# A decoder layer whose first product runs on x before its norm's root is known

## The chip, the cores and the metric

The kernel runs on one core of one Trainium2 chip. A core has TensorE (PE, matrix products and transposes, results in PSUM banks), VectorE (DVE), ScalarE (ACT) and GpSimd (POOL), which run side by side, each through its own instructions in order, and wait for one another by semaphores. SyncE (SP) issues most transfers between the chip's memory and the on-chip memory; ACT and POOL issue some. The metric is the device time of one execution in microseconds (us), the median of several.

## The reference, cut to what matters

One layer of a hybrid decoder: 256 prompt rows and 8 rows of new tokens, 2048 wide. Both start with a root-mean-square norm, and the normed rows go through one wide product, whose columns are split among attention, the gates and a state-space (SSM) branch:

```python
def rms_norm(x, w):
    y = x * lax.rsqrt(jnp.mean(x * x, axis=-1, keepdims=True) + EPS)
    return y * w

def token_mixers(hn, ...):            # hn = rms_norm(x, norm_mix_pre)
    proj = jnp.einsum('bld,de->ble', hn, lw['w_in'])
    q, k, v, z, xbc, dt_raw, gates = jnp.split(proj, SPLITS, axis=-1)
    xbc_act, new_conv = causal_conv(xbc, conv_in, conv_w, conv_b)    # columns X, B and C
    dt = softplus(dt_raw + dt_bias); a = -exp(a_log)                 # decays
    ...
```

The root of a row is one number for that row. So (x w r) W = r ((x w) W): it can be put on the product's result. The columns called B (1024 of them, for 8 groups) are the first that the kernel computes, 512 at a time, then C, then the 64 columns of dt (in 128), then X.

## The kernel before, in words

**Layout.** Activations stand transposed: a chunk is 128 of the 2048 channels on the partitions by 264 columns (256 prompt rows and 8 sample rows). There are 16 chunks. Products are of fp32 accuracy from parts: an operand is split into a high part, rounded to fp32r (a cast on ACT), and a low part, the difference (a subtraction on DVE). Each 128 x 128 block of weights then takes three matmuls: high by high (L192), high by the low part of x (L195), low by high (L196).

**The helper `gemm` (L147 to L198)** computes 512 columns: for each four chunks it loads 1 MB of raw weights (tile `raw`, 3 buffers, SP's queue, L163), casts `hi` and `lo` in halves of 1024 elements (L178 and L180 when they are tied behind given instructions, else L182 and L183; 4 buffers each), and runs 24 matmuls for each half, into four PSUM banks of tag `g` (5 banks; small transposes use 3 banks of tag `s`). One product of 512 columns is 192 matmuls.

**The start.** x comes in rows, in halves of 1024 columns (L230); sample rows, identity and norm vector go by ACT's queue (L231 to L233), small vectors by POOL's. In a block whose order is kept as written for PE, ACT and DVE (L265 to L304): idle matmuls on zeros (`busy`), transposes of x by fours (`turn`, L275), of the norm vector (L285) and the sample rows (L287), copies of the results into `XR` (L283, L290, L292, L297), sums of squares (L279, L281, L288, L293), the root by Newton steps on DVE (helper `rsqrt`, L98 to L116), and its broadcast over partitions by transposes (L302). Then each chunk is normalised: `xf = XR * w_pre * root` on DVE (L310), `XH` a cast on ACT (L92), `XL` on DVE (L93). The first product (columns B) runs on them, its weight casts tied behind the chunks' (L312, L313).

**What sets the order.** Outside the kept block a scheduler orders each engine's instructions by priorities and buffers; weight loads and casts get a higher priority, so they run ahead as far as buffers come free. `tc.issue_after` ties an instruction behind another. `mm0` holds the first product's matmuls; small vectors are transposed behind mm0[16] (L319 to L329).

**After the first product**, `conv` (L339 to L351) takes each result by ACT and DVE, `decays` (L353) computes a product of 128 columns and a long chain on its 64 rows, with a result that goes out to memory and comes back broadcast (tile `bc`, L482 to L488). It is called after the first product of B. The SSM branch (L499 and on) uses it after the products of C and X.

Of the kernel before, what the change touches and what calls it, by code (L numbers as in the profile page):

```python
# [32 lines left out]
def build(tc, I, O, wbufs=(3, 4, 4), gbufs=5, sbufs=((3,), (1,), (3,)), woff=0, aux="gpsimd", rr=1.4, pr=1.2, su=2, sr=1.0, hb=5, xbb=2, x0g=(0, 1, 2, 3), x0st="sync"):  # L33
    nc = tc.nc
    V, S, G, PE = nc.vector, nc.scalar, nc.gpsimd, nc.tensor
    dma, st = nc.sync.dma_start, nc.gpsimd.dma_start
# [226 lines left out]
    V.memset(ss, 1.0)
    ET = mybir.EngineType
    with tc.manual_schedule(engines={ET.PE, ET.Activation, ET.DVE}):  # L265
        pw = sps()
# [5 lines left out]
        def turn(t, k):
            ps = gps()
            for c in range(4 * k, 4 * k + 4):
                PE.transpose(ps[:, (c % 4) * P:(c % 4 + 1) * P], xts[t][:, c * P:(c + 1) * P], ident)  # L275
            return XR[:, 4 * k:4 * k + 4, t * P:(t + 1) * P], ps[:, :].rearrange("p (c n) -> p c n", c=4)

        busy(7)
        S.activation(sq[:NS], xts[2][:NS], AF.Square, accum_out=ss[:NS, 2:3])  # L279
        for h in range(2):  # L280
            S.activation(sq[:, h * XC:h * XC + XC], xts[0][:, h * XC:h * XC + XC], AF.Square, accum_out=s4[:, h:h + 1])  # L281
            for k in (2 * h, 2 * h + 1):
                V.tensor_copy(*turn(0, k))  # L283
# [6 lines left out]
        S.copy(XR[:, :, NP:T], pn[:, 128:256].rearrange("p (c n) -> p c n", c=16))  # L290
        for k in range(2):
            S.copy(*turn(1, k))  # L292
        V.tensor_tensor_reduce(sv2, xts[1][:, XC:], xts[1][:, XC:], 1.0, 0.0, ALU.mult, ALU.add, s4[:, 3:4])  # L293
        s2 = s4.rearrange("p (t h) -> p t h", t=2)
        V.tensor_tensor(ss[:, 0:2], s2[:, :, 0], s2[:, :, 1], ALU.add)
        for k in range(2, 4):
            xr_end = S.copy(*turn(1, k))  # L297
# [1 line left out]
        rs = rsqrt(cp, [(lambda a: a, ss)], P, 3, 1.0 / D, EPS, "rx")
        rbx = gps()  # L300
        for t, n in enumerate((P, P, NS)):
            PE.transpose(rbx[:, t * P:t * P + n], rs[:n, t:t + 1].broadcast_to([n, P]), ident[:n, :n])  # L302
        busy(2)
        rbx = rbx[:, :T]  # L304
# [2 lines left out]
    first = {0: xr_end.ins}, {}
    for c in range(16):
        xf = til(A0, [P, T], "xf", 3)
        V.scalar_tensor_tensor(xf, xrs[c], w_pre[:, c:c + 1], rbx, ALU.mult, ALU.mult)  # L310
        a, b = split(xf, XH[c], XL[c])
        first[0][c + 1] = a.ins  # L312
        first[1][c - 1] = b.ins  # L313
# [39 lines left out]
    def decays():  # L353
# [72 lines left out]
    for g in range(8):  # L426
        if g % 4 == 0:
            for nm, c0 in (("B", C_B), ("C", C_C)):
                pss = pss0 if g == 0 and nm == "B" else gemm(win, [(c0 + g * P, 512)], 16, X)
                for i in range(4):  # L430
                    cid = (c0 - C_X) // P + g + i
                    t = til(A2, [P, NP], "bc" + nm, 5)
                    conv(pss[i], cid, t)
# [730 lines left out]
```

## Time and profile before

| | before |
|---|---|
| median of 3 runs | 2142.59 us (2141.12 to 2143.07) |
| the profiled execution | 2147.37 us, of it the span 2145.6 us |
| mean granted clock of TensorE | 0.995 |
| PE, DVE, ACT busy | 99%, 64%, 52% |

Line numbers such as L192 are those of the kernel before. A tile's name stands without its buffer number. In the timeline a row is start, busy time, engine, line, operation, output and inputs, shape, count, and in brackets how long the engine stood idle before it and what ended that; rows of the same kind that follow one another are joined, with their count. "128*128 128x264" on a matmul is the weight block and the moving operand. The span's start is 0.

### The profile page before, as it was taken

To read this page: it belongs to the slowest core of one execution; us is meant where nothing else is said; L and a number is where in the kernel's file an instruction comes from. 1 tells how busy PE (TensorE), PEld (TensorE's weight loads), DVE (VectorE), ACT (ScalarE), POOL (GpSimd) and SP (SyncE) were. 2 spreads that over 40 slices of the span, in tenths; PEclk is the share of its full clock that TensorE was granted. 3 is DMA by queue.
4 is the path that set the end of the run, shared out by engine and by line. 5 is a ranking of instruction groups with operands and counts; after the bars stand their busy time and mean duration, and the time that the engine had idled before them with its cause. 6 is when DMAs were issued, how large, how long until landed. Compare 5 with 4: busy or idle time off the path is not lost.

```text
span 2145.6 us, 43115 instructions
## 1 busy us (share of the span) xinstructions
PE 2116.6 (99%) x17512; PEld 2083.6 (97%) x17512; DVE 1369.1 (64%) x2748; ACT 1105.0 (52%) x1969; POOL 234.2 (11%) x462
## 2 busy tenths in 40 slices
PE   8999999999999999999999999999999999999997
PEld 8999999999999999989999999999999999999997
DVE  7877777777689988867544554755455455544444
ACT  6555555555579877755533444554444444434442
POOL 1111011110123321233001100000000000000000
PEclk9999999999999999999999999999999999999998
DMA  7665655565577787787568975556555555565553
GB/s 254 208 195 191 192 192 177 192 192 192 190 259 251 254 287 252 266 280 260 179 208 183 219 256 184 167 186 206 193 188 188 190 195 195 185 212 177 177 177 100
DMA packets 214999, 442.50 MB, mean 206 GB/s; under 512 B 12000, under 2 KB 25840, under 8 KB 214280
## 3 DMA queue, kind: packets, MB, share of 16 engines
q1 hardware_dynamic: 192800, 370.91, 53.5%
q0 software_dynamic: 21664, 68.64, 9.7%
q8 instruction: 137, 2.24, 0.4%
q14 instruction: 62, 0.51, 0.1%
q10 hardware_dynamic: 336, 0.21, 0.0%
HBM read 402.81 MB, written 41.45 MB: 207 GB/s over the span
## 4 chain that ended last, share of the span: by engine, by line
PE 91%; DMA 5%; DVE 2%; issue 1%; ACT 1%; SPq 0%; POOL 0%; DVEq 0%; ACTq 0%; POOLq 0%
PE g L192 28%; PE g L196 28%; PE g L195 28%; DMA raw<-in_w_attn_branch 1%; DMA out_ssm_sample<-h 1%; DMA h<-in_state_ssm 1%; DMA ta_d<-tg 0%; PE w L735 0%; ACT hi L182 0%; PE w L728 0%; DMA xt<-in_x_prompt 0%; PE w L696 0%; PE s L499 0%; DMA raw<-in_w_in 0%; DVE lo L183 0%
## 5 line engine op out<-in xcount | busy, mean ns | idle before, releaser
L183 DVE TENSOR_TENSOR lo<-raw,hi 128x1024 fp32r<-128x1024 f32 (+1 forms) x632 | 765.4, 1214 | 595.5 <-ACT hi L182 594.2
L182 ACT CAST hi<-raw 128x1024 fp32r<-128x1024 f32 (+1 forms) x632 | 657.5, 1043 | 867.5 <-PE g L195 788.2
L192 PE MATMUL g<-XH,hi 128*128 128x264 f32 x2192 | 624.4, 288 | 2.3 <-ACT hi L182 1.1
L195 PE MATMUL g<-XL,hi 128*128 128x264 f32 x2192 | 622.0, 286 | 0.0
L196 PE MATMUL g<-XH,lo 128*128 128x264 f32 x2192 | 619.7, 287 | 1.7 <-DVE lo L183 1.0
L192 PEld LDWEIGHTS g<-XH,hi 128*128 128x128 f32 x2192 | 410.7, 188 | 6.9 <-issue 2.4
L195 PEld LDWEIGHTS g<-XL,hi 128*128 128x128 f32 x2192 | 411.4, 188 | 4.2 <-issue 3.5
L196 PEld LDWEIGHTS g<-XH,lo 128*128 128x128 f32 x2192 | 408.9, 188 | 5.3 <-issue 1.9
L195 PE MATMUL g<-HL,hi 128*128 128x264 f32 x1408 | 397.6, 284 | 0.0
L196 PE MATMUL g<-HH,lo 128*128 128x264 f32 x1408 | 397.0, 284 | 0.0
L192 PE MATMUL g<-HH,hi 128*128 128x264 f32 x1408 | 393.7, 285 | 0.0
L195 PEld LDWEIGHTS g<-HL,hi 128*128 128x128 f32 x1408 | 266.0, 189 | 0.9 <-DVE HL L956 0.8
L196 PEld LDWEIGHTS g<-HH,lo 128*128 128x128 f32 x1408 | 263.9, 188 | 0.0
L192 PEld LDWEIGHTS g<-HH,hi 128*128 128x128 f32 x1408 | 261.1, 188 | 0.0
L192 PE MATMUL g<-FH,hi 128*128 128x264 f32 x704 | 200.9, 286 | 0.0
L196 PE MATMUL g<-FH,lo 128*128 128x264 f32 x704 | 200.4, 285 | 0.0
L195 PE MATMUL g<-FL,hi 128*128 128x264 f32 x704 | 199.2, 283 | 0.0
L195 PE MATMUL g<-YL,hi 128*128 128x264 f32 x512 | 145.9, 286 | 0.8 <-DVE YL L93 0.8
L196 PE MATMUL g<-YH,lo 128*128 128x264 f32 x512 | 146.3, 287 | 0.0
L192 PE MATMUL g<-YH,hi 128*128 128x264 f32 x512 | 145.2, 288 | 0.9 <-ACT YH L92 0.9
L195 PEld LDWEIGHTS g<-FL,hi 128*128 128x128 f32 x704 | 132.8, 189 | 0.0
L192 PEld LDWEIGHTS g<-FH,hi 128*128 128x128 f32 x704 | 132.5, 188 | 0.0
(438 smaller groups left out, 2966.1 us busy)
## 6 DMA issues: line engine op xcount, KB each, us to landing
raw<-in_w_in SPq DMA_DIRECT2D x136, 1024.0 KB, 5.3
raw<-in_w_gate_up SPq DMA_DIRECT2D x88, 1024.0 KB, 5.1
raw<-in_w_down SPq DMA_DIRECT2D x44, 1024.0 KB, 5.1
raw<-in_w_ssm_branch SPq DMA_DIRECT2D x32, 1024.0 KB, 5.5
h<-in_state_ssm POOLq DMA_DIRECT2D x64, 256.0 KB, 5.7
out_ssm_sample<-h POOLq DMA_DIRECT2D x64, 256.0 KB, 5.2
raw<-in_w_attn_branch SPq DMA_DIRECT2D x32, 512.0 KB, 10.6
raw<-in_w_out SPq DMA_DIRECT2D x16, 1024.0 KB, 5.3
```

What stands on the lines that cost most here:

```text
L182: S.copy(hi[:, :, :w], r)
L183: V.tensor_tensor(lo[:, :, :w], r, fr(hi[:, :, :w]), ALU.subtract)
L192: ins = PE.matmul(ps[m][:, :T], wh, XH[kc], start=f, stop=False)
L195: PE.matmul(ps[m][:, :T], wh, XL[kc], start=False, stop=False)
L196: PE.matmul(ps[m][:, :T], wl, XH[kc], start=False, stop=l)
```

## The change

x is loaded by column pieces of 512 (both 128-row blocks in one transfer), laid between the first product's weight pieces. The block of kept order now holds the whole first product. After the idle matmuls, two chunks are transposed, and then a loop over eight passes b takes two chunks each: 16 matmuls with the high weights (4 result banks, 2 chunks, high and low part of x times w_pre, not normed), and after the first and the second bank's four a `turn` of a chunk of the next pass; then 8 matmuls with the low weights. `put` makes the two parts straight from the transposes' bank (ACT, then DVE), `keep_x` copies the raw chunk to `XR` (DVE for the odd chunks below 10, else ACT). Squares are summed for each piece behind passes 0 to 3 (ACT and DVE). Behind pass 4 the root is made: sums on DVE, a square root on ACT, a reciprocal and one Newton step on DVE, broadcast by transposes on PE and a copy on ACT (`rbs`). Behind passes 5 to 7 the chunks are normalised, two a pass, for the products that follow; behind the last one more, then the four results are scaled by the root (`BU`), then the rest. `decays` is called after the first product of C instead of B. The table that ACT loads at the start is the one of Sqrt, not Exp.

```diff
-    S.activation(warm, warm, AF.Exp)
+    S.activation(warm, warm, AF.Sqrt)
...
-    XC = 1024
-    for t in range(2):
-        for c0 in range(0, D, XC):
-            dma(xts[t][:, c0:c0 + XC], I["x_prompt"][t * P:t * P + P, c0:c0 + XC])
-    S.dma_start(xts[2][:NS], I["x_sample"])
...
+    load_x(0)
+    S.dma_start(xs8[:NS], I["x_sample"])
     S.dma_start(ident, I["consts"][:, 0:P])
     S.dma_start(N1[0:16], I["norm_mix_pre"].rearrange("(c p) -> c p", p=P))
+    load_raw(0, 2)
+    load_x(1)
+    load_x(2)
+    load_raw(1, 1)
+    load_x(3)
+    load_raw(2, 1)
...
+        def turn(c):
+            ps = sps()
+            for t in range(2):
+                PE.transpose(ps[:, t * P:t * P + P], xp[:, t, c * P:(c + 1) * P], ident)
+            PE.transpose(ps[:, NP:T], xs8[:NS, c * P:(c + 1) * P], ident[:NS, :NS])
+            return ps
+
+        def put(c, ps):
+            H, L = XU[c]
+            S.mul(H, ps[:, :T], w_pre[:, c:c + 1])
+            V.scalar_tensor_tensor(L, ps[:, :T], w_pre[:, c:c + 1], fr(H), ALU.mult, ALU.subtract)
+            return c, ps
+
+        def keep_x(c, ps):
+            (V.tensor_copy if c % 2 and c < 10 else S.copy)(XR[:, c, :], ps[:, :T])
...
+        def norm(c):
+            xf = til(A0, [P, T], "xf", 2)
+            V.scalar_tensor_tensor(xf, XR[:, c, :], w_pre[:, c:c + 1], rbs, ALU.mult, ALU.mult)
+            split(xf, XH[c], XL[c])
...
+        for b in range(8):
+            lo = low(b, hi)
+            for m in range(4):
+                for k in range(2):
+                    for x in range(2):
+                        mm = PE.matmul(pss0[m][:, :T], hi[:, k, m * P:(m + 1) * P], XU[2 * b + k][x], start=b + k + x == 0, stop=False)
...
+                if m < 2 and b < 7:
+                    a = put(2 * b + 2 + m, turn(2 * b + 2 + m))
+                    if m == 0:
+                        hi2 = high(b + 1)
+                    keep_x(*a)
+            for m in range(4):
+                for k in range(2):
+                    PE.matmul(pss0[m][:, :T], lo[:, k, m * P:(m + 1) * P], XU[2 * b + k][0], start=False, stop=b + k == 8)
+            hi = hi2
+            if b < 4:
...
+                S.activation(sq[:, 0:512], xb[:, 0], AF.Square, accum_out=s4[:, 0, b:b + 1])
+                V.tensor_tensor_reduce(sq[:, 1024:1536], xb[:, 1], xb[:, 1], 1.0, 0.0, ALU.mult, ALU.add, s4[:, 1, b:b + 1])
+            if b == 0:
+                load_raw(3, 1)
+            if b == 4:
+                V.tensor_reduce(ss[:, 0:2], s4, mybir.AxisListType.X, ALU.add)
...
+                S.activation(rs, rx, AF.Sqrt)
+                V.tensor_scalar(rh, rx, -0.5, None, ALU.mult)
+                V.reciprocal(rs, rs)
+                V.tensor_tensor(rt, rs, rs, ALU.mult)
+                V.tensor_tensor(rt, rt, rh, ALU.mult)
+                V.scalar_tensor_tensor(rs, rt, 1.5, rs, ALU.add, ALU.mult)
+                rbx = sps()
+                for t, n in enumerate((P, P, NS)):
+                    PE.transpose(rbx[:, t * P:t * P + n], rs[:n, t:t + 1].broadcast_to([n, P]), ident[:n, :n])
+                S.copy(rbs, rbx[:, :T])
+            if b > 4:
+                for _ in range(2):
+                    norm(todo.pop(0))
+        norm(todo.pop(0))
+        for i in range(4):
+            V.tensor_tensor(BU[:, i, :], pss0[i][:, :T], rbs, ALU.mult)
+        pss0 = [BU[:, i, :] for i in range(4)]
+        for c in todo:
+            norm(c)
...
-    pss0 = gemm(win, [(C_B, 512)], 16, (XH, XL), behind=first)
...
-                if g == 0 and nm == "B":
+                if g == 0 and nm == "C":
                     dtT, tokm, ac, DF, dcol, dc1 = decays()
```

PE in the middle of the first product, before (XH and XL are the two parts of a normed chunk, hi and lo those of weights, g the result banks):

```order
L195 MATMUL g_350<-XL_9_91,hi_357 128x264
L196 MATMUL g_347<-XH_8_90,lo_358 128x264
L192 MATMUL g_347<-XH_10_92,hi_357 128x264
L195 MATMUL g_347<-XL_11_93,hi_357 128x264
L196 MATMUL g_347<-XH_10_92,lo_358 128x264
L196 MATMUL g_348<-XH_8_90,lo_358 128x264
L192 MATMUL g_348<-XH_10_92,hi_357 128x264
L195 MATMUL g_348<-XL_11_93,hi_357 128x264
L196 MATMUL g_348<-XH_10_92,lo_358 128x264
L196 MATMUL g_349<-XH_8_90,lo_358 128x264
```

Matmuls of the three kinds follow one another with nothing between them.

The same place after the change (xu2H and xu2L are the parts of the raw chunk 2 times w_pre, s a bank for transposes, xp and xs the rows of x):

```order
L338 MATMUL g_223<-xu2H_178,hi_258 128x264
L338 MATMUL g_223<-xu2L_179,hi_258 128x264
L338 MATMUL g_223<-xu3H_180,hi_258 128x264
L338 MATMUL g_223<-xu3L_181,hi_258 128x264
L293 MATMUL s_298<-ident_67,xp_134 128x128 x2
L294 MATMUL s_298<-ident_67,xs_43_135 128x8
L338 MATMUL g_224<-xu2H_178,hi_258 128x264
L338 MATMUL g_224<-xu2L_179,hi_258 128x264
L338 MATMUL g_224<-xu3H_180,hi_258 128x264
L338 MATMUL g_224<-xu3L_181,hi_258 128x264
```

The matmuls are the same in number; the order goes bank by bank with high weights, and the turns of the next pass's chunks now stand between them.

PE at the end of pass 4 after the change (rxy is the root; before, these transposes stood ahead of the product):

```order
L348 MATMUL g_225<-xu9H_192,lo_424 128x264
L348 MATMUL g_226<-xu8H_190,lo_424 128x264
L348 MATMUL g_226<-xu9H_192,lo_424 128x264
L368 MATMUL s_478<-ident_67,rxy_470 128x128 x2
L368 MATMUL s_478<-ident_67,rxy_470 128x8
L338 MATMUL g_223<-xu10H_194,hi_436 128x264
L338 MATMUL g_223<-xu10L_195,hi_436 128x264
```

The root's transposes stand behind the pass's low matmuls and ahead of the whole of pass 5.

ACT at the end of the first product, before:

```order
L92 CAST XH_22_104<-xf_319 128x264
L178 CAST hi_473<-raw_467 128x1024
L92 CAST XH_24_106<-xf_323 128x264
L92 CAST XH_26_108<-xf_327 128x264
L178 CAST hi_527<-raw_525 128x1024
L92 CAST XH_28_110<-xf_331 128x264
L92 CAST XH_30_112<-xf_335 128x264
L178 CAST hi_531<-raw_525 128x1024
L182 CAST hi_669<-raw_667 128x2x128
```

Each weight cast stands behind the two chunks before it, and the next product's casts (hi_669 on) come last.

The same after the change (hi_749, hi_753 and hi_807 are weights of the next product, s_539 and s_552 the banks of the turned chunks 14 and 15):

```order
L299 ACTIVATE xu14H_202<-s_539,w_pre_165 128x264
L308 CAST hi_545<-raw_290 128x1024
L182 CAST hi_749<-raw_747 128x1024
L182 CAST hi_753<-raw_747 128x1024
L182 CAST hi_807<-raw_805 128x1024
L304 COPY XR_172<-s_539 128x264
L299 ACTIVATE xu15H_204<-s_552,w_pre_165 128x264
L304 COPY XR_172<-s_552 128x264
```

Three casts of the next product's weights moved in ahead of the copy of chunk 14 and the high part of chunk 15.

DVE at the same place after the change (lo_750 to lo_812 belong to the next product; BU are the scaled results):

```order
L313 TENSOR_TENSOR lo_583<-raw_290,hi_545 128x1024
L318 SCALAR_TENSOR_TENSOR xf_609<-XR_172,w_pre_165,s6t_123 128x264
L183 TENSOR_TENSOR lo_750<-raw_747,hi_749 128x1024
L183 TENSOR_TENSOR lo_754<-raw_747,hi_753 128x1024
L183 TENSOR_TENSOR lo_808<-raw_805,hi_807 128x1024
L93 TENSOR_TENSOR XL_13_95<-xf_609,XH_12_94 128x264
L318 SCALAR_TENSOR_TENSOR xf_613<-XR_172,w_pre_165,s6t_123 128x264
L183 TENSOR_TENSOR lo_812<-raw_805,hi_811 128x1024
L93 TENSOR_TENSOR XL_15_97<-xf_613,XH_14_96 128x264
L318 SCALAR_TENSOR_TENSOR xf_617<-XR_172,w_pre_165,s6t_123 128x264
L93 TENSOR_TENSOR XL_17_99<-xf_617,XH_16_98 128x264
L375 TENSOR_TENSOR BU_128<-g_223,s6t_123 128x264
```

Each xf is now followed by its own XL, with only low casts between, where before two chunks' steps stood between the two.

## Rows read from the trace of the kernel before

**Rows 1.** The page's busy shares, and its chain of waits by engine

```profile
PE 2116.6 (99%) x17512; PEld 2083.6 (97%) x17512; DVE 1369.1 (64%) x2748; ACT 1105.0 (52%) x1969; POOL 234.2 (11%) x462
...
PE 91%; DMA 5%; DVE 2%; issue 1%; ACT 1%; SPq 0%; POOL 0%; DVEq 0%; ACTq 0%; POOLq 0%
```

**Rows 2.** Stretch, length, busy PE, PEld, DVE, ACT, POOL, granted clock, DMA share, GB/s

```profile
16.40:41.00 24.60, 23.87 (x190) 23.11 (x191) 22.33 (x47) 13.21 (x26) 0.00 (x0) 1.00 0.59 214
```

**Rows 3.** Waits of 0 to 120 us: total, times, longest

```profile
PE g L302 <- DVE rxy L115: 1.2, 1, 1.2
PE g L192 <- ACT hi L182: 1.1, 1, 1.1
...
PE g L196 <- DVE lo L180: 0.7, 1, 0.7
```

**Rows 4.** Timeline of the start, 0 to 18 us

```profile
1.40 1.28 ACT L79 ACT_TABLE_LOAD   x1 [1.40 <-PEq L1156]
...
1.88 0.44 ACTq L233 DMA_DIRECT2D N<-in_norm_mix_pre  x1
...
9.20 1.15 PE L287 MATMUL s<-ident,xt 8*128 8x8 f32 x16
...
10.58 1.23 DVE L293 CUSTOM_DVE_ANT_0 sv<-xt 128x1024 f32<-128x1024 f32 x1 [0.19 <-DMA xt<-in_x_prompt]
...
13.23 0.16 DVE L115 SCALAR_TENSOR_TENSOR rxy<-rxt,rxy 128x3 f32<-128x3 f32 x1
...
16.38 0.75 PE L192 MATMUL g<-XH,hi 128*128 128x264 f32 x4
```

**Rows 5.** Tiles N and xt, from issue to landing

```profile
DMA to landing us min/median/max: 5.8/5.8/5.8
...
DMA to landing us min/median/max: 4.3/6.3/8.4
```

**Rows 6.** Timeline of PE in the first product

```profile
33.43 0.65 PE L192 MATMUL g<-XH,hi 128*128 128x264 f32 x4
33.92 0.65 PE L195 MATMUL g<-XL,hi 128*128 128x264 f32 x4
```

**Rows 7.** Timeline of PE around transposes between matmuls

```profile
74.07 0.28 PE L196 MATMUL g<-XH,lo 128*128 128x264 f32 x1
74.28 0.27 PE L386 MATMUL s<-ident,dtT 64*128 64x64 f32 x1
...
74.71 0.28 PE L195 MATMUL g<-XL,hi 128*128 128x264 f32 x1
...
110.52 0.29 PE L195 MATMUL g<-XL,hi 128*128 128x264 f32 x1
110.64 0.38 PE L457 MATMUL s<-ident,xs 128*128 128x128 f32 x2
...
110.98 0.28 PE L192 MATMUL g<-XH,hi 128*128 128x264 f32 x1
```

**Rows 8.** Timeline of ACT in the first product

```profile
33.38 0.41 ACT L92 CAST XH<-xf 128x264 fp32r<-128x264 f32 x1 [0.94 <-DVE xf L310]
33.70 1.05 ACT L178 CAST hi<-raw 128x1024 fp32r<-128x1024 f32 x1
```

**Rows 9.** Timeline of DVE in the first product

```profile
32.85 0.89 DVE L310 SCALAR_TENSOR_TENSOR xf<-XR,w_pre,g 128x264 f32<-128x264 f32 x2
33.65 0.78 DVE L93 TENSOR_TENSOR XL<-xf,XH 128x264 fp32r<-128x264 f32 x2
34.34 1.23 DVE L180 TENSOR_TENSOR lo<-raw,hi 128x1024 fp32r<-128x1024 f32 x1
```

**Rows 10.** Timeline of DVE and PE where the decays are used

```profile
83.19 0.41 DVE L401 COPY y<-s 64x256 f32<-64x256 f32 x1
...
92.07 1.66 DVE L488 TENSOR_SCALAR bc<-bc,ac 128x128 f32<-128x128 f32 x8 [0.79 <-DMA bc<-acT_d]
...
130.58 0.44 PE L499 MATMUL s<-bc,X 128*64 128x128 f32 x4
```

More of the change, by code (lines that the diff above doesn't have):

```diff
@@ L220, in build @@
     RS = til(RSp, [P, 4, NS, 48], "RS")
+    BU = til(RSp, [P, 4, T], "BU")
     A0 = pool("a0")
@@ L224, in build, with load_x, load_raw @@
     G.memset(wz, 0.0)
-    xts = [til(A0, [P, D], f"xt{t}") for t in range(3)]
+    xp = til(A0, [P, 2, D], "xp")
+    xs8 = til(A0, [P, D], "xs8")
     N1 = til(A0, [P, P], "N1")
-    XC = 1024
-    for t in range(2):
-        for c0 in range(0, D, XC):
-            dma(xts[t][:, c0:c0 + XC], I["x_prompt"][t * P:t * P + P, c0:c0 + XC])
-    S.dma_start(xts[2][:NS], I["x_sample"])
+    xv = I["x_prompt"].rearrange("(t p) d -> p t d", t=2)
+    raws = []
+    def load_x(k):
+        dma(xp[:, :, 512 * k:512 * k + 512], xv[:, :, 512 * k:512 * k + 512])
+    def load_raw(g, parts):
+        raws.append(til(wp, [P, 4, 512], "raw", wbufs[0]))
+        n = 4 // parts
+        for h in range(parts):
+            k0 = 4 * g + n * h
+            dma(raws[g][:, n * h:n * h + n, :], win[k0 * P:(k0 + n) * P, C_B:C_B + 512].rearrange("(k p) n -> p k n", p=P))
+    load_x(0)
+    S.dma_start(xs8[:NS], I["x_sample"])
     S.dma_start(ident, I["consts"][:, 0:P])
     S.dma_start(N1[0:16], I["norm_mix_pre"].rearrange("(c p) -> c p", p=P))
+    load_raw(0, 2)
[4 more added lines that the diff above has]
+    load_raw(2, 1)
     VR = til(A0, [P, P], "VR")
@@ L257, in build @@
     ss = til(cp, [P, 3], "ss")
-    s4 = til(cp, [P, 4], "s4")
+    s4 = til(cp, [P, 2, 4], "s4")
     XR = til(A0, [P, 16, T], "XR")
-    xrs = [XR[:, c, :] for c in range(16)]
     sq = til(A0, [P, D], "sq")
-    sv2 = til(A0, [P, XC], "sv2")
+    XU = [[til(A0, [P, T], f"xu{c}{x}", 1, F32R) for x in "HL"] for c in range(16)]
+    rbs = s6t.rearrange("p b c -> p (b c)")[:, 0:T]
     V.memset(ss, 1.0)
@@ L270, in busy @@
                 PE.matmul(pw[:, 0:NP], wz[:, 0:P], wz, start=True, stop=True)
[L272 to L283, printed above, removed]
@@ L284, in build @@
-        pn = sps()
+        def turn(c):
[9 more added lines that the diff above has]
+            return c, ps
@@ new lines, in keep_x, with high, low @@
+        def keep_x(c, ps):
+            (V.tensor_copy if c % 2 and c < 10 else S.copy)(XR[:, c, :], ps[:, :T])
+        def high(b):
+            hi = til(wp, [P, 2, 512], "hi", wbufs[1], F32R)
+            S.copy(hi, raws[b // 2][:, 2 * (b % 2):2 * (b % 2) + 2, :])
+            return hi
+        def low(b, hi):
+            lo = til(wp, [P, 2, 512], "lo", wbufs[2], F32R)
+            V.tensor_tensor(lo, raws[b // 2][:, 2 * (b % 2):2 * (b % 2) + 2, :], fr(hi), ALU.subtract)
+            return lo
@@ L285, in build @@
+        def norm(c):
+            xf = til(A0, [P, T], "xf", 2)
+            V.scalar_tensor_tensor(xf, XR[:, c, :], w_pre[:, c:c + 1], rbs, ALU.mult, ALU.mult)
+            split(xf, XH[c], XL[c])
+        S.activation(sq[:NS], xs8[:NS], AF.Square, accum_out=ss[:NS, 2:3])
+        busy(9)
+        pn = gps()
         PE.transpose(pn[:, 0:16], N1[:16], ident[:16, :16])
-        for c in range(16):
-            PE.transpose(pn[:, 128 + 8 * c:136 + 8 * c], xts[2][:NS, c * P:(c + 1) * P], ident[:NS, :NS])
@@ L288, in build @@
-        S.activation(sq[:, :XC], xts[1][:, :XC], AF.Square, accum_out=s4[:, 2:3])
         S.copy(w_pre, pn[:, 0:16])
[L290 to L297, printed above, removed]
@@ L298, in build @@
-        busy(3)
[L299 to L304, printed above, removed]
+        pss0 = [gps() for _ in range(4)]
+        xs = [put(c, turn(c)) for c in range(2)]
+        busy(3)
+        hi = high(0)
+        for a in xs:
+            keep_x(*a)
+        todo = list(range(16))
@@ new lines, in build @@
+        for b in range(8):
[4 more added lines that the diff above has]
+                        mm = PE.matmul(pss0[m][:, :T], hi[:, k, m * P:(m + 1) * P], XU[2 * b + k][x], start=b + k + x == 0, stop=False)
+                        if b == 1:
+                            mm0.append(mm.ins)
+                if m < 2 and b < 7:
+                    a = put(2 * b + 2 + m, turn(2 * b + 2 + m))
+                    if m == 0:
+                        hi2 = high(b + 1)
+                    keep_x(*a)
+            for m in range(4):
[3 more added lines that the diff above has]
+            if b < 4:
+                xb = xp[:, :, 512 * b:512 * b + 512]
+                S.activation(sq[:, 0:512], xb[:, 0], AF.Square, accum_out=s4[:, 0, b:b + 1])
[4 more added lines that the diff above has]
+                V.tensor_reduce(ss[:, 0:2], s4, mybir.AxisListType.X, ALU.add)
+                rx, rh, rt, rs = (til(cp, [P, 3], "rx" + k) for k in "xhty")
+                V.tensor_scalar(rx, ss, 1.0 / D, EPS, ALU.mult, ALU.add)
+                S.activation(rs, rx, AF.Sqrt)
[11 more added lines that the diff above has]
+                    norm(todo.pop(0))
@@ L305, in build @@
+        norm(todo.pop(0))
[4 more added lines that the diff above has]
+            norm(c)
     for c in range(0, 16, 4):
         st(xT_d[c:c + 4].rearrange("c p t -> p c t"), XR[:, c:c + 4, :])
[L307 to L313, printed above, removed]
@@ L318, in build @@
     ps = sps()
-    with tc.issue_after(mm0[16]):
+    with tc.issue_after(mm0[8]):
         for k in range(5):
@@ L326, in build @@
     ps = sps()
-    with tc.issue_after(mm0[16]):
+    with tc.issue_after(mm0[8]):
         PE.transpose(ps[:, 0:48], VR[:48], ident[:48, :48])
@@ L366, in decays @@
         V.scalar_tensor_tensor(e, u, -1.0, u, ALU.mult, ALU.max)
-        S.activation(e, e, AF.Exp, scale=-1.0)
+        e_act = S.activation(e, e, AF.Exp, scale=-1.0)
         V.tensor_scalar(s, e, 2.0, None, ALU.add)
@@ L378, in decays @@
         na = til(cp, [P, 1], "na")
-        S.activation(na[h_], hv[h_, 1:2], AF.Exp)
+        with tc.issue_after(e_act.ins):
+            S.activation(na[h_], hv[h_, 1:2], AF.Exp)
         V.tensor_scalar(na[h_], na[h_], -1.0, None, ALU.mult)
```

## The prediction

> **What bounds the kernel now.** I read the busy shares and the chain of waits first. TensorE is busy 99% of the span and makes up 91% of the chain that ended last [rows 1], so only three things can move the time: work added to or taken from PE's queue, a wait of PE, or the time at which PE starts real work. Next I read the table by stretches. From 16.4 to 41 us, the first product (192 matmuls), PE is busy 23.87 of 24.60 us, DVE 22.33 and ACT 13.21 at a granted clock of 1.00 [rows 2]: DVE is nearly as full as PE, so vector work added in this stretch soon stops PE. PE's waits of the first 120 us are short: 1.2 for the root, 1.1 and 0.7 for weights [rows 3]. The timeline of the start shows what stands ahead of the product: transposes and the root on DVE, and the first product matmul at 16.38 [rows 4].
>
> The sum is made against the profiled run, 2147.37 us (span 2145.6 and 1.8 around it). That is 4.8 above the median 2142.59 of the runs; at the end I take 4.8 off.
>
> **A: the start, -5.5.** The first transpose of the change needs the norm vector, the identity and the first column piece of x. The vector is issued at 1.88 [rows 4] and lands 5.8 later [rows 5]: 7.7. The x landings are 4.3 to 8.4 from issue [rows 5]; the first piece is issued first, so it is there at about the same time. Then 0.3 for the vector's transpose, two turns of 0.62 each (worked out in B): 9.25. On ACT, H of the second chunk, 0.41, and the high cast of the weights, 1.05, one behind the other [rows 8]: about 10.9 for the first product matmul, where 16.38 stood. Ends: -5.0 (first piece late by the median landing) and -5.8.
>
> **B: turns inside the product, +8.7, and root transposes, +0.6.** Matmuls of the product start 0.49/4 = 0.122 us apart [rows 6]. Fourteen turns now stand between them, each two transposes of 128 rows and one of the 8 sample rows. Two 128-row transposes put between matmuls stretch 110.52 to 110.98, which is 0.46 where two intervals would be 0.24: 0.22 extra [rows 7]. A lone transpose from 64 rows stretches 74.07 to 74.71, which is 0.64 against 0.24: 0.40 extra [rows 7]. The 8-row transposes among themselves took 1.15/16 = 0.07 each [rows 4]. So a turn costs between 0.22 + 0.07 = 0.29 and 0.22 + 0.40 = 0.62; times 14, 4.1 to 8.7. I take the upper end, because the 64-row row is the only one in which a short transpose stands between full matmuls, as here. The three root transposes were ahead of the product and are now in it: 0.3 to 0.9, I take 0.6.
>
> The row with 64 rows shows 0.40 us lost around one short transpose. The Trainium skill, TensorEngine Tiling (Array Packing), Key Properties, says that a change of tiling mode (other than a change of tile within it) drains TensorE. By it each 8-row transpose would cost like that row, and the sum would be as here; without it the turns cost 4.1 and the sum is 4.6 less. The trace agrees so far, with 0.40 against 0.11 for each of the 128-row ones.
>
> **C: the root after the fifth pass, +0.9.** Root transposes stand in PE's order behind the low matmuls of pass 4 and wait for DVE's last root instruction. Ahead of it on DVE, once the low cast of pass 4 is done: two L of 0.45 with a copy 0.35 and an H 0.41 on ACT between them, a reduction and a scaling (0.4), the Sqrt on ACT (0.25), then four small ones of 0.16 [rows 4] with their handing over, 0.8 (all estimates from that row's size): 3.1 in all. PE covers 8 x 0.122 = 0.98 of it, so 2.1 at most. At least 0, if DVE is far ahead. Per pass DVE's path is 0.45 + 0.40 + 0.41 + 0.45 + 0.36 + 0.69 (half of the 1.23 square plus its read [rows 4]) + 1.22 (low cast [rows 9]) = 4.0, PE's is 24 x 0.122 + 2 x 0.62 = 4.17; DVE starts about 2 us ahead, gains 0.2 a pass, and so covers about half: 0.9.
>
> In that path ACT's H, DVE's L and the copy of the same transposed chunk stand one behind another; no row of before shows three readers of one bank. The Trainium skill, PSUM — Partial Sum Buffer, section "PSUM bank collisions raise a hardware error", says that two engines, readers too, must not be at one bank and the same partitions at once, so a program has to order them. By it the path is the 4.0 above; without that order DVE would need its own 3.2 only and term C would be nothing, 0.9 off the sum.
>
> **D: DVE behind the root, +7.0.** This is the large term. From the root to the first of the four scalings BU, DVE has 7 low casts of 1.23, some 0.1 of it under the next one [rows 9], = 7.9 (four of them already of the next product), four L at 0.40 = 1.6, four small vectors 1.0 (estimate: under the 0.40 of a chunk each), seven chunks of norm at 0.40 + 0.35 = 0.75 (0.80 and 0.69 for two [rows 9]) = 5.2, one BU 0.4: 16.1. To it come waits in the order shown in the last order piece: each norm's own low part waits for ACT's cast of the same chunk (0.41 [rows 8] and the handing over, 0.5, times 7 = 3.5; before, two chunks stood between), L of chunk 13 behind a high cast and a copy on ACT (0.95 + 0.3 = 1.25), and L of chunk 15 behind H15, which stands behind four casts of 1.05 less 0.1 overlap [rows 8] = 3.8, of which DVE's small vectors and L14 hide some: 2.0. In all 22.85. PE has in the same stretch 93 matmuls = 11.4, four turns 2.5, root 0.6, small transposes 0.9 (seven at about a matmul's interval [rows 6]): 15.4. The next product runs its first bank for chunks 0 to 6 and then needs a second bank, which BU0 frees. So PE is short by 22.85 - 15.4 = 7.5 at most, and by 16.1 - 15.4 = 0.7 if every wait is filled. I take 7.0: some of the waits fall together with PE's own. Before, the same norm chain stood under PE at 22.33 of 24.60 [rows 2] because it had no L300, no copies and no squares beside it.
>
> **E: the decay product one product later, +1.0.** Its chain ended 83.19 + 0.41 and what needs it, the broadcast, had landed by 92.07 [rows 10]: 8.5 us; PE's first matmuls of the SSM branch that take it stand at 130.58 [rows 10], 38 us after. A product of 192 matmuls later is some 24 us [rows 2], so it still fits on PE's side, but the wait of DVE at the broadcast can hold low casts: 0 to 3, near the lower end. The wait of 1.1 at its weights [rows 3] recurs behind the other product at the same price: nothing. The wait of 0.7 for the low cast at the first product [rows 3] goes: **-0.7**. The new table load for Tanh falls on ACT, which is busy 13.21 of 24.60 [rows 2]: nothing, 1.3 [rows 4] if not covered.
>
> Sum: -5.5 + 8.7 + 0.6 + 0.9 + 7.0 + 1.0 - 0.7 = +12.0, so 2159.4 against the profiled run and 2154.5 against the median. With all low ends: -5.8 + 4.1 + 0.3 + 0 + 0.7 + 0 - 0.7 = -1.4; with all high ends: -5.0 + 8.7 + 0.9 + 2.1 + 7.5 + 3 + 1.3 = +18.5.
>
> **The rivals.** (1) Not slower: DVE's waits in D are filled, because ACT has half of the stretch free [rows 2] and runs ahead, and the turns cost their low end. This decides if DVE's stretch from root to BU0 stays within PE's 15.4; it speaks against it that 16.1 of pure work is above 15.4 already, and that ACT's four casts stand in front of H15 by the order. Price: the sum of the low ends, rounded to -1: 2141.6. (2) The turns are cheap, or DVE starves PE by half only: +12.0 less 4.6 for the first or less 3.5 for the second, less 7 to 8 with both: +4 to +8, of which both together, +4.5, gives 2147. For it speaks the 0.07 of the 8-row transposes among themselves [rows 4]. (3) The decay chain is late: its wait stands on DVE ahead of low casts, and PE loses the 3 of E, with C and the table at their ends too: +18, 2160.5. Against it speaks the slack from 92.07 to 130.58 [rows 10].
>
> **How the numbers follow.** A measurement of this kernel tells about 0.2%, 4.3 us, from no change. The forecast has 0.60, with its own range +7.5 to +16 (2150 to 2158.5); rival 1 has 0.14, half within 4.3 and half beyond (a gain of another 3 us would have to come from where my rows show none); rival 2 in its lowest form has 0.16, of which 0.06 within 4.3; rival 3 has 0.10. So faster 0.07, same 0.07 + 0.06 = 0.13, slower 0.60 + 0.10 + 0.10 = 0.80. The range 2144 to 2163 leaves out most of rival 1 and a little above rival 3.
>
> **What the changed profile would show.** A: the first product matmul at about 10.9; wrong if above 12. B: passes of the first product about 4.2 long while PE waits for nothing, with a gap of 0.4 around each 8-row transpose; wrong if the two turns add under 0.7 per pass. C: a wait of PE of about 0.9 at the root's transposes. D: waits of PE for low casts, XL and ACT's casts between about 45 and 57 us that add up to 7, and the second bank of the next product first written about 55; if they are under 2, the sum's large term is wrong and rival 1 or 2 holds. E: no PE wait from 100 us on that before did not have. If the first product ends before 36 us with no waits behind it, my forecast has the wrong sign.

## The result, and the profile after

| | before | after |
|---|---|---|
| median of 6 runs | 2142.83 us (2141.12 to 2147.40) | 2162.32 us (2158.49 to 2165.14) |
| ratio, 95% interval | | 1.0086 [1.0074, 1.0098] |
| profiled execution | 2147.37 us, span 2145.6 | 2165.00 us, span 2163.2 |

The change made the kernel slower, by 19.5 us in the medians and 17.6 us between the two profiled executions. The forecast was +12.0 (2154.6 for the median), with 2144 to 2163 as range. The page's busy shares and chain of the kernel after:

```profile
PE 2129.3 (98%) x17512; PEld 2091.2 (97%) x17512; DVE 1375.7 (64%) x2769; ACT 1115.4 (52%) x1996; POOL 238.9 (11%) x462
...
PE 93%; DMA 3%; DVE 2%; ACT 1%; issue 1%; SPq 0%; DVEq 0%; ACTq 0%; POOL 0%; POOLq 0%
```

PE is still the chain [rows 1]; the same 17512 instructions now end later. PE's timeline of the start and the first pass (start, busy time, engine, line, operation, tiles, shapes, count, idle time before):

```profile
8.30 0.20 PE L324 MATMUL g<-ident,N 16*128 16x16 f32 x1 [0.70 <-DMA N<-in_norm_mix_pre]
...
11.06 0.39 PE L338 MATMUL g<-xu0H,hi 128*128 128x264 f32 x1
...
11.53 0.28 PE L338 MATMUL g<-xu1L,hi 128*128 128x264 f32 x1
11.65 0.38 PE L293 MATMUL s<-ident,xp 128*128 128x128 f32 x2
11.97 0.22 PE L294 MATMUL s<-ident,xs 8*128 8x8 f32 x1
12.12 0.39 PE L338 MATMUL g<-xu0H,hi 128*128 128x264 f32 x1
12.35 0.29 PE L338 MATMUL g<-xu0L,hi 128*128 128x264 f32 x1
...
15.26 0.28 PE L338 MATMUL g<-xu2H,hi 128*128 128x264 f32 x1
```

The first product matmul stands at 11.06 where 16.38 stood [rows 4]. Around a turn, 11.53 to 12.35 is 0.82 us, where two matmul intervals are 0.24 [rows 6]: 0.58 for a turn. The root's transposes, behind pass 4:

```profile
32.56 0.55 PE L368 MATMUL s<-ident,rxy 128*128 128x128 f32 x3 [0.90 <-DVE rxy L365]
...
33.27 0.28 PE L338 MATMUL g<-xu10L,hi 128*128 128x264 f32 x1
```

PE's waits from 0 to 140 us (total, times, longest) put two more behind it, both in the last pass:

```profile
PE g L348 <- DVE lo L313: 1.9, 1, 1.9
...
PE g L338 <- ACT xu15H L299: 1.1, 1, 1.1
PE s L368 <- DVE rxy L365: 0.9, 1, 0.9
```

What they wait for is in the timelines of ACT and DVE:

```profile
36.85 0.38 ACT L304 COPY XR<-s 128x264 f32<-128x264 f32 x1 [0.56 <-DVE xu13L L300]
...
40.21 2.94 ACT L182 CAST hi<-raw 128x1024 fp32r<-128x1024 f32 x3
...
43.33 0.48 ACT L299 ACTIVATE xu15H<-s,w_pre 128x264 fp32r<-128x264 f32 x1
```

```profile
34.72 0.49 DVE L300 SCALAR_TENSOR_TENSOR xu12L<-s,w_pre,xu12H 128x264 fp32r<-128x264 f32 x1 [1.18 <-ACT xu12H L299]
...
45.22 0.43 DVE L93 TENSOR_TENSOR XL<-xf,XH 128x264 fp32r<-128x264 f32 x1 [0.48 <-ACT XH L92]
...
46.88 1.22 DVE L313 TENSOR_TENSOR lo<-raw,hi 128x1024 fp32r<-128x1024 f32 x1
48.02 0.49 DVE L318 SCALAR_TENSOR_TENSOR xf<-XR,w_pre,s6t 128x264 f32<-128x264 f32 x1
48.42 3.49 DVE L183 TENSOR_TENSOR lo<-raw,hi 128x1024 fp32r<-128x1024 f32 x3
...
55.37 1.44 DVE L375 TENSOR_TENSOR BU<-g,s6t 128x264 f32<-128x264 f32 x4
```

From the end of the root on DVE (32.4) to the end of the first BU (55.8) are 23.4 us; the forecast had 22.85. And a thing that no row of before shows, in the table by stretches (length, busy PE, PEld, DVE, ACT, POOL, granted clock, DMA share, GB/s):

```profile
46.00:48.00 2.00, 0.24 (x2) 0.02 (x1) 1.52 (x3) 0.41 (x1) 0.00 (x0) 1.00 0.76 270
...
50.00:52.00 2.00, 2.00 (x11) 1.77 (x9) 2.00 (x3) 0.00 (x0) 0.00 (x0) 0.56 0.96 357
...
56.00:58.00 2.00, 2.00 (x11) 2.00 (x11) 1.52 (x5) 1.07 (x5) 0.00 (x0) 0.50 0.14 38
...
60.00:62.00 2.00, 2.00 (x17) 2.00 (x16) 0.84 (x2) 0.32 (x2) 0.00 (x0) 0.88 0.00 0
```

PE stood nearly idle from 46 to 48 us; from 50.3 to 60.5 us the granted clock was 0.50 (1.2 GHz), and matmuls started 0.22 us apart instead of 0.122.

To place the loss I count the 264-column matmuls into result banks in both traces and take how much later the n-th starts than in the kernel before (the lag). After: first -5.3, 191st +6.8, 335th (before: at 62 us) +10.9, 1400th (212 us) +16.4, and 15 to 18 from there on. So there are two losses: 16.2 us from the first to the 335th, and 5.5 from there to the 1400th.

### The profile page after: what moved, and what is told of

The parts are those of the page before. It is cut to its first block, busy times and chain, and to the rows that moved or that the text cites. A ratio compares the mean times of both kernels' runs of the same rounds, so it can differ in the third digit from the quotient of the medians.

```text
span 2163.2 us, 43146 instructions
## 1 busy us (share of the span) xinstructions
PE 2129.3 (98%) x17512; PEld 2091.2 (97%) x17512; DVE 1375.7 (64%) x2769; ACT 1115.4 (52%) x1996; POOL 238.9 (11%) x462
## 4 chain that ended last, share of the span: by engine, by line
PE 93%; DMA 3%; DVE 2%; ACT 1%; issue 1%; SPq 0%; DVEq 0%; ACTq 0%; POOL 0%; POOLq 0%
PE g L196 29%; PE g L192 29%; PE g L195 28%; DMA raw<-in_w_attn_branch 2%; DVE lo L183 1%; PE g L338 1%; PE w L801 1%; PE w L794 0%; PE w L762 0%; PE s L565 0%; ACT hi L182 0%; DMA bc<-acT_d 0%; PE s L536 0%; PE s L523 0%; PE s L531 0%
## 5 line engine op out<-in xcount | busy, mean ns | idle before, releaser
L192 PE MATMUL g<-XH,hi 128*128 128x264 f32 x2128 | 612.0, 289 | 1.2 <-ACT hi L182 0.6
L195 PE MATMUL g<-XL,hi 128*128 128x264 f32 x2128 | 610.4, 288 | 0.5 <-DVE XL L93 0.4
L196 PE MATMUL g<-XH,lo 128*128 128x264 f32 x2128 | 607.8, 288 | 2.4 <-DVE lo L183 2.3
L195 PEld LDWEIGHTS g<-XL,hi 128*128 128x128 f32 x2128 | 403.4, 190 | 5.1 <-issue 3.3
L192 PEld LDWEIGHTS g<-XH,hi 128*128 128x128 f32 x2128 | 402.5, 190 | 5.9 <-issue 2.4
L196 PEld LDWEIGHTS g<-XH,lo 128*128 128x128 f32 x2128 | 400.7, 189 | 6.6 <-DVE lo L183 3.8
```

The costliest lines, as they stand in the source:

```text
L192: ins = PE.matmul(ps[m][:, :T], wh, XH[kc], start=f, stop=False)
L195: PE.matmul(ps[m][:, :T], wh, XL[kc], start=False, stop=False)
L196: PE.matmul(ps[m][:, :T], wl, XH[kc], start=False, stop=l)
```

## The experiments

All lags are against the profiled kernel before; ratios are against the runs of before that were taken with each kernel, whose medians were 2142.8 to 2144.3.

| kernel | lag first | lag 335th | lag 1400th | median us | ratio, 95% interval |
|---|---|---|---|---|---|
| after | -5.3 | 10.9 | 16.4 | 2162.3 | 1.0086 [1.0074, 1.0098] |
| e1 before, late decays | 0.0 | -2.3 | 0.8 | 2145.2 | 1.0005 [0.9995, 1.0015] |
| e2 after, early decays | -5.1 | 12.8 | 13.7 | 2157.3 | 1.0064 [1.0049, 1.0079] |
| e3 full rows | -2.1 | 14.0 | 20.8 | 2164.1 | 1.0092 [1.0077, 1.0107] |
| e4 filled | -5.2 | 10.4 | 13.1 | 2155.0 | 1.0053 [1.0038, 1.0068] |
| e8 POOL | -5.2 | 8.6 | 12.2 | 2154.7 | 1.0048 [1.0033, 1.0063] |
| e5 pairs | -5.2 | 8.9 | 13.8 | 2156.5 | 1.0053 [1.0036, 1.0070] |
| e6 hold | -5.4 | 9.6 | 12.3 | 2157.2 | 1.0060 [1.0041, 1.0079] |
| e9 full rows early | -2.3 | 13.0 | 18.0 | 2163.5 | 1.0087 [1.0072, 1.0102] |
| e12 filled more | -5.2 | 9.5 | 16.1 | 2157.4 | 1.0061 [1.0046, 1.0076] |
| e13 no low | -5.2 | 4.7 | 9.9 | 2153.6 | 1.0041 [1.0026, 1.0056] |
| e14 full rows third | -3.4 | 11.5 | 16.9 | 2159.3 | 1.0075 [1.0058, 1.0091] |

**e1: the late decays alone, in the kernel before.**

```diff
-                if g == 0 and nm == "B":
+                if g == 0 and nm == "C":
                     dtT, tokm, ac, DF, dcol, dc1 = decays()
```

> The kernel before, with the decay product called after the first product of C instead of B, nothing else. Theory: the changed kernel lost 10.9 us up to the 335th product matmul (start and first product) and another 5.5 us from about 117 to 210 us, and this second loss is the later decay product alone: this kernel is 4.5 to 6.5 us slower than before, with a wait of PE of 1 to 2 us at the SSM branch's first matmuls for the broadcast's scaling on DVE. Rival, the forecast's own figure: the later call costs 0 to 2 us, and the second loss came from the shift of the first one against the transfers.

Measured: 1.0005 [0.9995, 1.0015], and 0.8 us at the 1400th matmul. My theory fell: alone, the later call costs what the forecast gave it (+1.0). The run also shows a trap in my counting: its lag is -2.3 at the 335th, because the decays' small matmuls and waits come later in the count, and it takes 3.1 us back by the 1400th. Every kernel with late decays has these 3.1 in its lags. Against e1 the changed kernel is 13.2 us late at the 335th, and of the second loss of 5.5 only 2.4 are left.

**e2: the changed kernel with early decays** (the same line turned back).

> The changed kernel with the decay product called after B again. Theory: the second loss of 5.5 us goes, but a product of 128 columns needs a normed chunk every 0.37 us where DVE makes one in 1.3 us, so PE waits longer behind the first product: lag behind the kernel before at the 335th product matmul 13 to 16 us instead of 10.9, in all 0 to 3 us faster than the changed kernel. Rival: the chunks keep ahead, the first lag stays 11 and the whole 5.5 is won.

The lag at the 335th is 12.8, just under the 13 to 16 expected, and without the shift of the count about the changed kernel's 13.2. Two things stand against each other in its trace: the longer wait for normed chunks at the decay product is there, but the first BU comes 3.0 us sooner, since the low casts ahead of it are the small ones (128x256) of the decay product. PE's waits and DVE in e2:

```profile
PE g L192 <- ACT XH L92: 2.9, 3, 1.4
```

```profile
52.39 1.44 DVE L375 TENSOR_TENSOR BU<-g,s6t 128x264 f32<-128x264 f32 x4
```

From there to the 1400th it loses 1.0 where the changed kernel loses 2.4 (shift taken off); at the 1400th it is 2.6 ahead. The forecast's E is thus 0.8 alone and 2.6 in this kernel. In the changed kernel PE's waits from 60 to 220 us show part of it, with DVE's last step on the broadcast ahead of all:

```profile
PE s L565 <- DVE bc L556: 1.5, 1, 1.5
PE g L192 <- ACT hi L182: 0.6, 1, 0.6
PE g L192 <- ACT RS L410: 0.5, 1, 0.5
PE g L196 <- DVE lo L183: 0.4, 1, 0.4
```

That it isn't a fixed price the other kernels show: with the shift taken off, the second loss is -0.4 in e4 and e6, 0.6 in e8, 1.8 in e5 and e9, 2.1 in e13, 2.2 in e14, 3.5 in e12 and 3.7 in e3. In e5, e8, e12 and e13 PE waits 1.9 to 2.1 us for a weight cast on ACT at 81 to 86 us, and in e5, e12 and e13 the granted clock then stands at 0.50 for 3.4 us; in e3, e9 and e14 it waits 1.0 to 2.1 us for the broadcast, as the changed kernel does; in e4 and e6 it does neither. Each edit moved the scheduler's order there, and which of these moves made the difference stays open.

**e3, e9, e14: turns of three equal transposes.**

```diff
-            PE.transpose(ps[:, NP:T], xs8[:NS, c * P:(c + 1) * P], ident[:NS, :NS])
+            PE.transpose(ps[:, NP:NP + P], xs8[:, c * P:(c + 1) * P], ident)
```

They differ in how rows 8 to 127 are filled, and when the sample rows are loaded (e3: all zeroed first; e9: 24 rows of x, zeros on the rest; e14: below).

```diff
+    V.memset(xs8[0:32, 0:1024], 0.0)
+    G.memset(xs8[0:32, 1024:], 0.0)
     S.dma_start(ident, I["consts"][:, 0:P])
     S.dma_start(N1[0:16], ...)
+    S.dma_start(xs8[:NS], I["x_sample"])
+    V.memset(xs8[32:64], 0.0)
+    V.memset(xs8[64:], 0.0)
```

> The changed kernel with the 8 sample rows padded by zeros to 128, so that a turn is three transposes from 128 rows. Theory (a change of the row shape between matmuls costs about 0.2): a turn costs 0.34 to 0.38 instead of 0.58 us, a pass of the first product 3.6 to 3.7 instead of 4.06, 14 turns give back 3 us up to the root; as PE then waits sooner for DVE, some of that comes back as longer waits at the root and behind it: lag at the 335th matmul 8 to 11. Rival (three instructions cost what they cost, whatever the rows): a turn stays at 0.55 to 0.6, lag unchanged.

> The changed kernel with a turn of three transposes from 128 rows as in the run before, but with the sample rows loaded first, and the other rows filled by 24 rows of x and zeros, so that the start is not later. First product matmul at 10.8 to 11.3 us; a turn costs 0.34 us instead of 0.58. Theory: DVE's path of 4.0 us a pass and its chain behind the root set the end, so PE only waits more (at the root 2 to 3 us instead of 0.9) and the lag at the 335th matmul is 10 to 11, as in the changed kernel. Rival: the turns' cost adds to the time, 14 x 0.24 = 3.4 us are won, lag 7.5 to 8.5.

> The changed kernel with turns of three transposes from 128 rows, the other rows set to zero ahead of the sample rows' transfer, which is issued third on its queue behind identity and norm vector. First product matmul at 11 to 13 us; a turn at 0.34 us instead of 0.58. Theory: the DVE chain sets the end, so of the 3.4 us won by the turns at most 1.5 is left in the lag at the 335th matmul, counted from the first product matmul (16.2 us from the first matmul's lag to the 335th's in the changed kernel; here 14.7 to 16.2), and PE waits 2 to 3 us at the root. Rival: all of it is left, 12.5 to 13.3.

In e3 and e9 the start came 3 us later (in e3 the sample rows landed late, in e9 identity and norm vector), and the granted clock stood at 0.50 behind it (6.8 us in e3, 3.4 in e9). Both missed the lag that was expected (14.0 and 13.0) and tell little of the sum (e9 kept 15.4 of the changed kernel's 16.2 us between the first and the 335th matmul). A turn of e14 in PE's timeline:

```profile
25.73 0.29 PE L342 MATMUL g<-xu7L,hi 128*128 128x264 f32 x1
25.85 0.38 PE L297 MATMUL s<-ident,xp 128*128 128x128 f32 x2
26.07 0.27 PE L298 MATMUL s<-ident,xs 128*128 128x128 f32 x1
26.09 0.37 PE L342 MATMUL g<-xu6H,hi 128*128 128x264 f32 x1
26.30 0.29 PE L342 MATMUL g<-xu6L,hi 128*128 128x264 f32 x1
```

From 25.73 to 26.30 is 0.57, less 0.24: 0.33 for a turn instead of 0.58. The larger transpose is the cheaper one, by 0.25. This has the sign of the Trainium skill's rule that a change of tiling mode drains TensorE (TensorEngine Tiling (Array Packing), Key Properties); that the 8-row transpose is such a change, no run here shows. But the lag from the first to the 335th matmul went from 16.2 to 14.9 only, though 14 turns gave back 3.5, as the theory had it (14.7 to 16.2). The rest went into longer waits of PE, among them the one at the root, where 0.9 stood (2 to 3 were expected):

```profile
PE s L372 <- DVE rxy L369: 1.7, 1, 1.7
```

**e4, e12: PE kept busy in its waits** by products of zeros added into the result banks, six in the last pass (e4), and six more in the next product (e12).

```diff
+            if b == 7:
+                for _ in range(4):
+                    PE.matmul(pss0[3][:, 0:NP], wz[:, 0:P], wz, start=False, stop=False)
...
+                        for _ in range(fill.get(kc, 0) if m == 0 else 0):
+                            PE.matmul(ps[m][:, 0:NP], zz[0][:, 0:P], zz[0], start=False, stop=False)
```

> The changed kernel with six products of zeros added into the result banks in the last pass (two where PE waited 1.07 us, four where it waited 1.92 us), so that PE has work in those waits. Theory: the granted clock of 0.50 from 50.3 to 60.5 us followed that idling; with fillers it stays at 1.00, and since DVE frees the second bank at 55.4 us, only the time behind that is won: lag at the 335th product matmul 8 to 9.5 us instead of 10.9. Rival: DVE's chain sets the whole stretch, the clock stays at 1.00 and the lag at 10.5 to 11. If the clock falls all the same, the run tells nothing of its price.

> The run with products of zeros in PE's waits, with six more of them in the waits of the next product (four ahead of chunk 4's low part, one each ahead of chunks 5 and 6), where the first fillers had still left 1.7 and 0.3 us idle and the clock fell from 55.0 to 58.4 us. Theory (the clock after the first BU costs PE its half speed, 0.10 us for each matmul, since PE is the bound there): the clock stays at 1.00 throughout and the lag at the 335th product matmul falls from 10.4 to 8.3 to 9.2 us. Rival (DVE is the bound there too): lag 10 to 10.6 with the clock at 1.00.

The table by stretches, e4 and then e12:

```profile
50.00:55.00 5.00, 2.72 (x15) 1.88 (x15) 4.52 (x7) 0.41 (x1) 0.00 (x0) 1.00 1.01 375
55.00:60.00 5.00, 4.88 (x26) 4.40 (x27) 3.57 (x10) 2.05 (x7) 0.00 (x0) 0.66 0.25 74
```

```profile
50.00:55.00 5.00, 4.52 (x25) 3.50 (x24) 4.52 (x7) 0.41 (x1) 0.00 (x0) 1.00 1.02 377
55.00:60.00 5.00, 4.75 (x37) 4.45 (x35) 3.56 (x10) 2.06 (x7) 0.00 (x0) 1.00 0.24 73
```

In e4 the clock held to 55 us and then fell for 3.4 us, behind a further wait of 1.7 us; the lag went from 10.9 to 10.4, not to 8 to 9.5, and since the clock fell all the same, this run gives it no price. In e12 it stayed at 1.00 through this stretch (the fall at 87 us lies behind the 335th matmul), and the lag is 9.5, between the theory's 8.3 to 9.2 and the rival's 10 to 10.6. What the low clock cost is read behind the first BU. PE in the changed kernel:

```profile
56.12 0.42 PE L192 MATMUL g<-XH,hi 128*128 128x264 f32 x1
...
60.51 0.29 PE L195 MATMUL g<-XL,hi 128*128 128x264 f32 x1
```

These 4.39 us hold twenty intervals of 0.22, which at 0.122 would be 2.44: 2.0 us lost. From 56 us to the 335th matmul PE waits for nothing. In e12 nothing is lost behind the first BU, but that BU came 0.7 us later than the changed kernel's (55.37):

```profile
56.06 1.44 DVE L385 TENSOR_TENSOR BU<-g,s6t 128x264 f32<-128x264 f32 x4
```

So the low clock costs 2.0 us here, 0.10 for each matmul as the theory had it, and e12's 1.4 is that less the later BU. Ahead of the first BU, the low clock cost nothing that these runs show: DVE (4.52 of 5.00 us busy) set the pace, and with the full clock its BU came no sooner. Of the 7 us by which e4 is faster than the changed kernel in the median, 0.5 come by the 335th matmul and 2.8 from the second loss; the other 4 lie behind 212 us, and I have no cause for them.

**e5, e6, e8, e13: DVE's chain behind the root.**

e5 norms the chunks in pairs (two xf, then the two splits), e6 ties the next product's first three casts behind the copy of chunk 15, e8 subtracts XL on POOL, and e13 splits only from the eighth normed chunk on.

```diff
+    behind=({0: kx.ins, 2: kx.ins, 4: kx.ins}, {}) if g == 0 else None      # e6
...
-            split(xf, XH[c], XL[c])
+            split(xf, XH[c], XL[c], E=G)                                    # e8
...
+            if c < 7:                                                       # e13
+                S.copy(XH[c], xf)
+            else:
+                split(xf, XH[c], XL[c])
```

> The changed kernel with the chunks normed in pairs: two xf, then two XL, so that the cast of one runs under the xf of the other. Theory (DVE's chain sets the end): three to six waits of 0.48 go ahead of the first BU and more behind it, 1.5 to 2.7 us; lag at the 335th product matmul 8 to 9.5 us. Rival (the waits are filled by PE's own lateness): lag 10.5 to 11.

> The changed kernel with the first three weight casts of the next product tied behind the copy of chunk 15, so that the high part of chunk 15 no longer stands behind them on ACT. Theory (a part of DVE's chain is its wait for that high part): PE's wait of 1.07 us for H15 goes, the last low cast of the first product comes 1.5 to 2.5 us sooner than 46.9, the first BU sooner than 55.4 by as much; lag at the 335th product matmul 8.5 to 9.5 us. Rival (the casts only change places, the next product then waits for them): lag 10.5 to 11.5.

> The changed kernel with the low parts XL of the normed chunks subtracted on POOL instead of DVE, nothing else. Theory: from the root to the first BU, DVE's chain (23.4 us in the changed kernel) sets the end of the first product; without seven XL (0.35 each) and the wait before each (0.48) it is 5.8 us shorter, the second bank of C comes at about 50 instead of 55.4 us, the clock does not fall, and the lag at the 335th product matmul is 4 to 7 us instead of 10.9. Rival: ACT's casts and the transposes hold PE, DVE only waits with it; then the lag stays at 9.5 to 11.

> The changed kernel without the low part of the first seven normed chunks (their XL are zeros, written at the start; this part of the sum is left out), so that DVE does seven subtractions less between the root and the first BU and waits for none of ACT's casts there. Theory (DVE's chain sets the end of the first product): first BU at 49 to 51 us instead of 55.4, PE's waits from 42 us on under 2 us, lag at the 335th product matmul 4 to 7 us instead of 10.9. Rival (PE's lateness comes from the casts on ACT or the transfers): first BU after 53, lag over 9.

The first BU of e5 and the end of e13's chain, in DVE's timeline:

```profile
53.92 1.44 DVE L376 TENSOR_TENSOR BU<-g,s6t 128x264 f32<-128x264 f32 x4
```

```profile
48.59 0.89 DVE L318 SCALAR_TENSOR_TENSOR xf<-XR,w_pre,s6t 128x264 f32<-128x264 f32 x2
49.40 1.21 DVE L183 TENSOR_TENSOR lo<-raw,hi 128x1024 fp32r<-128x1024 f32 x1
50.53 0.48 DVE L318 SCALAR_TENSOR_TENSOR xf<-XR,w_pre,s6t 128x264 f32<-128x264 f32 x1
50.94 1.44 DVE L380 TENSOR_TENSOR BU<-g,s6t 128x264 f32<-128x264 f32 x4
```

e13 decides it: with seven subtractions and their waits gone, the first BU comes 4.4 us sooner and the lag at the 335th falls from 10.9 to 4.7, within the expected 4 to 7; the clock stays at 1.00 through 60 us, so that its 2.0 are won as well. (PE's waits of 1.2 and 0.8 us there are not under the 2 us expected.) e5 wins 2.0 with the first BU 1.45 sooner, as expected; the low clock lasts 3.4 us there. e6 missed its reason: H15 came sooner, but the casts then stood ahead of the normed chunks' casts. ACT, DVE and PE's wait in e6:

```profile
42.70 2.94 ACT L179 CAST hi<-raw 128x1024 fp32r<-128x1024 f32 x3
```

```profile
45.98 0.43 DVE L93 TENSOR_TENSOR XL<-xf,XH 128x264 fp32r<-128x264 f32 x1 [3.19 <-ACT XH L92]
```

```profile
PE g L348 <- DVE lo L313: 4.2, 1, 4.2
```

Its first BU is later (56.1), and its lag is still 1.3 smaller than the changed kernel's; the low clock lay earlier, from 47.6 to 54.5 us, under DVE's chain, so that PE behind it ran at full speed: 0.7 lost and 2.0 won. e8 fell short of its 4 to 7: the first BU came at 52.7, not about 50, the clock fell all the same (50.5 to 57.3 us), and POOL became the one that PE waits for. PE's waits, POOL and DVE in e8:

```profile
PE g L195 <- POOL XL L93: 2.7, 2, 2.0
```

```profile
44.85 5.18 POOL L93 TENSOR_TENSOR XL<-xf,XH 128x264 fp32r<-128x264 f32 x2
```

```profile
49.36 0.96 DVE L318 SCALAR_TENSOR_TENSOR xf<-XR,w_pre,s6t 128x264 f32<-128x264 f32 x1 [0.63 <-POOL XL L93]
```

## Why the prediction was right or wrong

The direction was right, and so was the mechanism; the size was short by 5.6 us against the profiled pair and by 7.5 in the medians. The measured median lies above the forecast's own range (2150 to 2158.5) and at the upper end of the wide one. The nearest number, 2160.5, is the third rival's, but its mechanism came only in part (E), so that its nearness is chance. Term by term, to the 335th matmul against e1 (13.2 in all; the forecast had 11.0 without E):

- **A** forecast -5.5, measured -5.35: the first product matmul came at 11.06 for 10.9, since the norm vector landed some 0.5 us later than taken.
- **B** forecast +8.7, measured 14 x 0.58 = 8.1. The 64-row row [rows 7] was the right neighbour; e14 shows that it was the short transpose that cost (it changed rows and columns together, 8x8 to 128x128). Root transposes +0.6, measured 0.75 (33.27 less 31.37 in the trace, less two intervals and the wait).
- **C** forecast +0.9, measured 0.90. So close a hit is luck: the value was a half taken between 0 and 2.1, and the same wait was 1.7 in e14. The three readers of a transposed chunk did stand one behind another: ACT's copy waited 0.56 us for DVE's low part. This agrees with the order that the Trainium skill asks for (PSUM — Partial Sum Buffer, section "PSUM bank collisions raise a hardware error"); no run here leaves the order out.
- **D**, with the old wait that goes, forecast 7.0 - 0.7 = +6.3, measured +8.8 as the rest of 13.2. This step failed in size. Its chain came out at 23.4 us for 22.85, and e13 and e5 show that it is what PE waits for. The sum of the chain's waits (6.7 for 6.75) is partly luck: five round trips of 0.48 stood where seven were forecast, and the 1.18 for chunk 12's high part, which was not in it, made up for them. Missing was the end of it: I let PE run at full speed from the first BU on, but the granted clock stood at 0.50 after PE's idling, and that cost 2.0 us behind the first BU. With the 0.55 of the longer chain this is the 2.5 by which the term was short; the chunks normed later held PE up no more.
- **E** forecast +1.0, of the range 0 to 3. Alone 0.8 (e1); in the changed kernel another 2.4 stand between the 335th and the 1400th, of which 1.0 come with early decays too (e2). PE's wait of 1.5 for DVE's work on the broadcast is the part named in the third rival. So the forecast's mechanism and a part of this rival's both came.

These make 16.4 us by 212 us. The last 1.2 to the profiled 17.6 are the net of gains and losses behind that; behind 860 us the clock stood at 0.50 for 13.7 us instead of 10.2, in short falls at places that differ from one profiled kernel to the next, so I give them no cause. The two medians lie another 1.9 apart, which the spread of runs of each kernel (6 to 7 us) covers.

The first rival (DVE's waits are filled) fell: DVE never caught up. The second (cheap turns) fell on 0.58 a turn; and e14 shows that cheaper turns would not have helped much, because the same DVE chain then ends later than PE (its first BU stands 43.5 us behind its first product matmul, where 44.3 stood). No version came out that beats the kernel before: even with DVE's work lightened as in e13, which leaves out a part of the sum, the ratio is 1.0041 [1.0026, 1.0056], and turns and root in the product cost 9.7 against 5.35 won at the start.

## What to carry to other kernels

An early start of the bound engine is worth only what the engines that feed it can keep up: count their work over the whole stretch, with each round trip between two engines (0.48 us for a cast of 0.41 here), before counting the head start. Putting a factor on the result removes one wait and adds a second full set of splits; where the vector engine is already 90% busy, that set is the price. And a wait of the matmul engine can be paid twice, once as idle time and once more in the clock behind it, but only where nothing else is slower at that moment.

## What was not expected of the hardware

- The granted clock fell to 0.50 after a stretch with PE busy 0.24 of 2.0 us, 2 us after its end, for 10.2 us; matmuls of 264 columns then started 0.22 us apart. It cost 2.0 us behind the first BU and nothing that the runs show ahead of it. In the kernel before, waits of 1.2 and 1.1 us [rows 3] left it at 1.00 (its first fall stands at 950 us).
- A transpose of 8 rows between matmuls of 128 rows costs 0.25 us more than one of 128 rows (0.58 and 0.33 for a turn; 8x8 against 128x128).
- POOL's subtraction of 128x264 took 0.75 to 2.6 us each, against 0.43 on DVE, and a DVE xf under it 0.96 instead of 0.49.
- The square root of 128x3 on ACT took 0.21 us.
